# Values phase of a retention and HGRN2 step: a second plain pair, sums on DVE, tiles at multiples of 512 bytes

## The chip, the core and the metric

The kernel runs on one core of a Trainium2 chip. The core has a matrix engine (TensorE, PE in the profile), a vector engine (VectorE, DVE), a scalar engine (ScalarE, ACT), GpSimd (POOL) and an engine that here issues DMAs (SyncE, SP). Each takes its instructions strictly in the order in which they stand; they wait for each other by semaphores. The metric is the device time of one execution in microseconds, the median over runs.

## The reference

One decoder layer over a prompt of 2,048 tokens and a batch of 8 new tokens, width 1,024, in float32. The input is RMS-normalised and multiplied by `w_in` (1,024 x 4,096), whose columns are eight groups of 512: for retention q, k, v and gate, for HGRN2 q, forget gate, value and gate. Each branch has four heads of 128.

```python
h = rmsnorm(x, norm_g)
p = (h @ w_in).astype(jnp.float32)
rq, rk, rv, rg, hq, hf, hi, hgate = jnp.split(p, 8, axis=-1)
...
o_ret, s_ret_new = chunked_decay_recurrence(rq, rk, rv, log_gamma, s_ret)
o_hg, s_hg_new = chunked_decay_recurrence(hq_act, kin, hi, logf, s_hg)
...
y = x + concatenate([norm(o_ret) * silu(rg), norm(o_hg) * silu(hgate)]) @ w_out
```

Retention has rotary positions and a fixed decay per head; HGRN2 has a forget gate per token and channel. Outputs are the normalised y for prompt and new tokens and the new states.

## The kernel before

**Numbers in two parts.** Every operand of the large products is split into a rounded high part (a copy on ACT into `float32r`) and a low part (a subtraction on DVE): `hi_lo` (lines 100 to 102, and `split`). `three` (line 287) then does three matmuls, high by high, high by low, low by high, into one PSUM accumulation.

**The values phase** (lines 164 to 491, up to about 212 us) computes the two value groups, `rv` and `hi`, for all tokens and writes them to DRAM. Tokens are taken in eight pairs of 128-token chunks, in the order `V_ORDER = [4, 5, 6, 7, 2, 3, 0, 1]`. The product of a pair is a 2 x 2 block product: two token chunks, two halves of the inner dimension, two groups of columns. The first pair is done plainly, eight block products (96 matmuls of 512 columns, loop at lines 437 to 455), while the weights arrive. The other seven are done by a Strassen-Winograd scheme with seven block products (84 matmuls, `v_pair`, `PRODUCTS`), for which sums of weight blocks (T1 to T4, made once by `wv_comb` from raw tiles `wvr`, four adds per k on POOL, each then split) and sums of token blocks (S1 to S4, `tok_ops`, four adds per pair on POOL, split by `s_split`) are needed. The decode tokens' values are 32 more matmuls (`decode_values`).

**Normalisation.** `stats(i)` loads two rows of 128 x 1,024 of the prompt one after the other into the single buffer `xn`, squares and sums them on ACT, and POOL makes the inverse root (`rsqrt_mean`). A plain pair needs it only at the eviction, as a scale per row. A Strassen pair needs it along the columns: `spread(i)` builds two diagonal matrices `dg` on DVE, PE multiplies them by ones (line 236), ACT copies the result to SBUF, and `tok_ops` multiplies the transposed tokens by it.

**Buffers.** Raw loads (`rawp`, six buffers of 4 KB per partition) are shared by weights, tokens and S sums; pools are laid out in SBUF in the order in which they are opened. In the built program `xh0` begins at byte 11,168 of a partition, `xl0` at 27,808, the weight buffers `wh` at 77,728 and the first T tile at 128,320: 416, 160, 416 and 320 past a multiple of 512. A row of an x tile is 520 numbers, 2,080 bytes. The output product's `wo` tiles take the places of the x tiles, with rows of 4,096 bytes; its other operand stands in the weight buffers.

**After the values phase** come sixteen units, one per half of the tokens, branch and head: projections (line 530) with the recurrence of the unit before woven in by `merge` (line 970). `merge` takes a list of steps with weights and places each at its share of the unit's projection work; what counts is the order that comes out of it. Nothing reorders PE's instructions; on the other engines a scheduler sets the order at build time. For an HGRN head (`hgrn_rec`) the steps are `scores0`, `scores(1)`, `scores(3)`, `scores3`, then transposes of k (`k0`, `k1`, line 635), state updates (`u0`, `u1`), outputs and output transposes. Between the scores a chain runs: ACT copies k and q (`keep`, lines 764 and 765), POOL multiplies k (line 754) and DVE multiplies q (line 757) by decays, in place; `scores3` (matmuls at lines 829 and 834) reads both, and `k0` reads k after POOL's last multiplication. At the end stands the output product (line 1107), with the decode work among it (lines 911 and 953).

Of the kernel before, what the change touches and what calls it, by code (L numbers as in the profile page):

```python
# [41 lines left out]
def step_kernel(ctx, tc, a, out):  # L42
# [27 lines left out]
    pool.memset(mhalf, -0.5)  # L70

# [21 lines left out]
    rst = const.tile([P, T - 512], F32, name="rst")  # L93
    dq, dk, df, dg_ = (const.tile([P, 8, NB], F32, name=f"d{n}") for n in "qkfg")
# [74 lines left out]
    side = [xp.tile([P, KT, 512 + NB], F32R, tag=f"x{t}1", name=f"wv_{t}") for t in "hl"]  # L169
# [33 lines left out]
    def stats(i):  # L203
        p = V_ORDER[i]
        ms = sm.tile([P, 2], F32, tag="ms", name=f"ms{p}")
        for j in range(2):
            c = 2 * p + j
            if i == 1:
                r = wp.tile([P, D], F32, tag="w" + "hl"[j], name=f"xn{c}")
            else:  # L210
                r = vq.tile([P, D], F32, tag="xn", name=f"xn{c}")
            sp.dma_start(r, a["x_prompt"][0, c * P : (c + 1) * P, :])
            act.activation(r, r, AF.Square, accum_out=ms[:, j : j + 1])
        rsqrt_mean(rs_all[:, 2 * p : 2 * p + 2], ms, D, EPS)

    def stats0():
        p = V_ORDER[0]
        ms = sm.tile([P, 4], F32, tag="ms4", name="ms0", bufs=1)
        for n, tag in enumerate(("s1", "u2", "u3", "vo")):
            c, h = 2 * p + n % 2, n // 2  # L220
            r = vq.tile([P, GW], F32, tag=tag, name=f"xn0{n}", bufs=2 if tag == "vo" else 1)
            sp.dma_start(r, a["x_prompt"][0, c * P : (c + 1) * P, h * GW : (h + 1) * GW])
            act.activation(r, r, AF.Square, accum_out=ms[:, n : n + 1])
        pool.tensor_tensor(ms[:, 0:2], ms[:, 0:2], ms[:, 2:4], op=ALU.add)
        rsqrt_mean(rs_all[:, 2 * p : 2 * p + 2], ms[:, 0:2], D, EPS)

    spread_to = {}

    def spread(i):
        p = V_ORDER[i]  # L230
        pt = ps_tr.tile([P, 2, P], F32, tag="tr", name=f"prs{p}")
        for j in range(2):
            c = 2 * p + j
            dg = vq.tile([P, P], F32, tag="dg", name=f"dg{c}", bufs=2)
            dve.tensor_scalar(dg, ident, rs_all[:, c : c + 1], None, op0=ALU.mult)
            pe.matmul(pt[:, j], ones, dg, start=True, stop=True)
        if p >= 2:
            dst = rst[:, (p - 2) * 256 : (p - 1) * 256]
        else:
            dst = vq.tile([P, 256], F32, tag="rb", name=f"rb{p}", bufs=2)  # L240
# [5 lines left out]
    def tok_ops(i):  # L246
        r0, r1 = xr[i]
        rb = spread_to[i]
        for j, r in enumerate((r0, r1)):
# [5 lines left out]
            hi_lo(xh0[:, 4 * j : 4 * j + 4, slot(i)], xl0[:, 4 * j : 4 * j + 4, slot(i)], r)  # L255
# [3 lines left out]
        pool.tensor_tensor(s1, a21, a22, op=ALU.add)  # L259
        pool.tensor_tensor(s2, s1, a11, op=ALU.subtract)  # L260
        pool.tensor_tensor(s3, a11, a21, op=ALU.subtract)
        pool.tensor_tensor(s4, a12, s2, op=ALU.subtract)
# [71 lines left out]
    def tok_load0(k0, tag):  # L334
        r = vq.tile([P, GW], F32, tag=tag, name=f"x0r{k0}", bufs=2 if tag == "vo" else 1)
        x0r[k0] = r.rearrange("p (k t) -> p k t", k=2)
        sp.dma_start(x0r[k0], a["x_t"][V_ORDER[0], :, k0 : k0 + 2])

    def x_split0(k):
        h, l = xh0[:, k, :256], xl0[:, k, :256]  # L340
        r = x0r[k - k % 2][:, k % 2]
# [7 lines left out]
    def wv_load(k, cuts=1):  # L349
        wr[k] = rawp.tile([P, 2, GW], F32, tag="raw", name=f"wvr{k}")  # L350
# [86 lines left out]
    for kk in range(4):  # L437
# [5 lines left out]
        if kk == 3:  # L443
            spread(1)
# [774 lines left out]
```

## Time and profile before

| | us |
|---|---|
| three runs | 1144.94, 1144.24, 1141.24 (median 1144.24) |
| profiled execution, whole | 1144.43 |
| its span, first to last instruction | 1142.6 |
| PE busy | 1095.2 (96%) |
| DVE, ACT, POOL busy | 665.9, 377.5, 270.7 |
| granted TensorE clock, mean | 0.989 |

Times in the views are microseconds from the span's start. A row of the waits names the waiting engine, tile and line, then whom it waited for, the total, how often, and the longest. Matmuls are pipelined: one of 512 columns is shown as about 394 ns long, but the next starts some 230 ns later, so the pace is read from groups (time of a group over its count).

### The profile page before, as it was taken

To read this page: it belongs to the slowest core of one execution; us is meant where nothing else is said; L and a number is where in the kernel's file an instruction comes from. 1 tells how busy PE (TensorE), PEld (TensorE's weight loads), DVE (VectorE), ACT (ScalarE), POOL (GpSimd) and SP (SyncE) were. 2 spreads that over 40 slices of the span, in tenths; PEclk is the share of its full clock that TensorE was granted. 3 is DMA by queue.
4 is the path that set the end of the run, shared out by engine and by line. 5 is a ranking of instruction groups with operands and counts; after the bars stand their busy time and mean duration, and the time that the engine had idled before them with its cause. 6 is when DMAs were issued, how large, how long until landed. Compare 5 with 4: busy or idle time off the path is not lost.

```text
span 1142.6 us, 21543 instructions
## 1 busy us (share of the span) xinstructions
PE 1095.2 (96%) x9062; PEld 922.9 (81%) x9062; DVE 665.9 (58%) x1048; ACT 377.5 (33%) x777; POOL 270.7 (24%) x268
## 2 busy tenths in 40 slices
PE   5889899999999999999999999999999999999997
PEld 3568688898998998998988888788788878878785
DVE  7856667566447447455757644644545685566343
ACT  6553323223323233322533322332322442233311
POOL 5733342013014005103302302401410420010011
PEclk9889899999999999999999999999999999999999
DMA  6355425821220221221443122122022275777431
GB/s 247 112 181 187 138 74 156 270 84 38 74 75 21 75 65 49 74 56 40 136 142 94 40 77 75 36 69 82 26 77 58 76 199 173 214 241 234 153 126 61
DMA packets 96305, 125.77 MB, mean 110 GB/s; under 512 B 4968, under 2 KB 69736, under 8 KB 96208
## 3 DMA queue, kind: packets, MB, share of 16 engines
q1 hardware_dynamic: 96064, 124.13, 34.7%
q8 instruction: 71, 1.16, 0.4%
q10 hardware_dynamic: 144, 0.26, 0.1%
q14 instruction: 26, 0.21, 0.1%
HBM read 93.11 MB, written 31.26 MB: 109 GB/s over the span
## 4 chain that ended last, share of the span: by engine, by line
PE 63%; issue 11%; POOL 11%; DVE 7%; ACT 4%; DMA 3%; SPq 0%; POOLq 0%; DVEq 0%; ACTq 0%
PE py L1107 15%; PE pjg L530 10%; PE pjfh L530 8%; PE pv L289 8%; PE pjqh L530 8%; POOL kh L754 5%; POOL qr L585 2%; DMA xn<-in_x_prompt 2%; PE pjqr L530 2%; ACT kepth L764 2%; POOL kr L585 1%; PE pur L642 1%; PE por L657 1%; PE par L699 1%; PE por L659 1%
## 5 line engine op out<-in xcount | busy, mean ns | idle before, releaser
L530 PE MATMUL pjg<-xh,w_h 128*128 128x512 f32 (+2 forms) x320 | 116.9, 365 | 0.0
L530 PE MATMUL pjg<-xh,w_l 128*128 128x512 f32 (+2 forms) x320 | 111.9, 350 | 0.0
L530 PE MATMUL pjg<-xl,w_h 128*128 128x512 f32 (+2 forms) x320 | 111.6, 349 | 0.0
L1107 PE MATMUL py<-woh,oc_h 128*128 128x512 f32 x256 | 100.8, 394 | 0.0
L1107 PE MATMUL py<-woh,oc_l 128*128 128x512 f32 x256 | 99.8, 390 | 0.0
L1107 PE MATMUL py<-wol,oc_h 128*128 128x512 f32 x256 | 99.6, 389 | 0.0
L101 ACT ACTIVATE w_h<-wr 128x1024 fp32r<-128x1024 f32 x48 | 50.8, 1058 | 100.6 <-PE pjg L530 48.8
L757 DVE TENSOR_TENSOR qth<-qth,fph 128x512 f32<-128x512 f32 x48 | 50.7, 1057 | 44.9 <-ACT kepth L765 43.2
L102 DVE TENSOR_TENSOR w_l<-wr,w_h 128x1024 fp32r<-128x1024 f32 x48 | 62.8, 1309 | 22.2 <-ACT w_h L101 22.0
L764 ACT ACTIVATE kepth<-kh 128x1024 f32<-128x1024 f32 x24 | 25.5, 1061 | 127.4 <-POOL kh L754 127.4
L530 PEld LDWEIGHTS pjg<-xh,w_l 128*128 128x128 f32 x320 | 60.1, 188 | 8.6
L530 PEld LDWEIGHTS pjg<-xl,w_h 128*128 128x128 f32 x320 | 60.4, 189 | 6.7
L530 PEld LDWEIGHTS pjg<-xh,w_h 128*128 128x128 f32 x320 | 60.3, 188 | 6.5
L754 POOL TENSOR_TENSOR kh<-kh,fph 128x512 f32<-128x512 f32 x48 | 56.8, 1184 | 32.1 <-ACT kepth L764 28.1
L97 POOL TENSOR_SCALAR orsr<-omsr,pk 128x4 f32<-128x4 f32 x16 | 4.3, 269 | 250.9 <-ACT jkr L663 250.9
L530 PE MATMUL pjfh<-xh,w_h 128*128 128x512 f32 (+2 forms) x160 | 58.9, 368 | 0.0
L530 PE MATMUL pjkr<-xh,w_h 128*128 128x512 f32 (+2 forms) x160 | 58.4, 365 | 0.0
L530 PE MATMUL pjqr<-xh,w_h 128*128 128x512 f32 (+2 forms) x160 | 58.4, 365 | 0.0
L530 PE MATMUL pjqh<-xh,w_h 128*128 128x512 f32 (+2 forms) x160 | 57.8, 361 | 0.0
L1107 PEld LDWEIGHTS py<-woh,oc_h 128*128 128x128 f32 x256 | 48.1, 188 | 10.4
L1107 PEld LDWEIGHTS py<-woh,oc_l 128*128 128x128 f32 x256 | 48.0, 188 | 10.2
L530 PE MATMUL pjqr<-xh,w_l 128*128 128x512 f32 (+2 forms) x160 | 56.1, 351 | 0.0
(485 smaller groups left out, 2851.4 us busy)
## 6 DMA issues: line engine op xcount, KB each, us to landing
wr<-in_w_in SPq DMA_DIRECT2D x48, 512.0 KB, 4.4
v_dram<-vo SPq DMA_DIRECT2D x32, 256.0 KB, 3.1
v<-v_dram SPq DMA_DIRECT2D x16, 512.0 KB, 4.8
or<-o_dram SPq DMA_DIRECT2D x16, 512.0 KB, 5.2
xrc<-in_x_prompt SPq DMA_DIRECT2D x16, 512.0 KB, 3.8
out_y_prompt<-yc SPq DMA_DIRECT2D x15, 512.0 KB, 2.6
xn<-in_x_prompt SPq DMA_DIRECT2D x14, 512.0 KB, 4.1
xr<-in_x_t SPq DMA_DIRECT2D x14, 512.0 KB, 4.3
```

The source lines that it names most:

```text
L101: act.activation(h, src, AF.Copy)
L102: dve.tensor_tensor(l, src, h.bitcast(F32), op=ALU.subtract)
L289: pe.matmul(ps, xx, ww, start=(first and n == 0), stop=(last and n == 2))
L530: pe.matmul(ps, ww[:, kk], x[:, k, b0 : b0 + n], start=(k == 0 and i == 0), stop=(k == KT - 1 and i == 2),)
L585: pool.tensor_tensor(dst[:, tt], t1[:, :n], t2[:, :n], op=ALU.add)
L642: pe.matmul(pu[:, j], ksb[g][:, j], vcol(4 * g + j), start=True, stop=True)
L657: pe.matmul(po[:, j], A[:, c], vcol(c), start=True, stop=src is None)
L659: pe.matmul(po[:, j], qcol(c), src, start=False, stop=True)
L754: pool.tensor_tensor(kv[:, :, 0, :], kv[:, :, 0, :], two[:, :, 1:2].to_broadcast([P, nb, b]), op=ALU.mult)
L757: dve.tensor_tensor(qv[:, :, 1, :], qv[:, :, 1, :], two[:, :, 0:1].to_broadcast([P, nb, b]), op=ALU.mult)
L764: act.activation(ss[:, 512:], k[:, :HALF], AF.Copy)
L1107: pe.matmul(ps, o[:, kk], w[:, k % 4, i * 512 : (i + 1) * 512], start=(k == 0 and n == 0), stop=(k == KT - 1 and n == 2),)
```

## The change

The diff touches the values phase, the layout of tiles, and one table of weights:

- The pair after the first is plain as well (192 plain matmuls, then six Strassen pairs of 84). Its tokens come in small tiles (`tok_load0(1, k)`), and each of its four outputs is accumulated over all k in turn, with the decode values between.
- All eight raw weight tiles have a buffer of their own (two of them in the pool of the split weights). The sums of weights are no longer between the loops of the first pair; `wv_comb` comes after it, and its adds, like those of `tok_ops`, are on DVE instead of POOL. One `stats` serves the first pair like the others.
- `spread` is cut in two: `spread_dg` (diagonals on DVE) a step earlier, `spread` (matmul and copy) where it was. For the last pairs and the decode it stands in other places.
- For Strassen pairs below the sixth only the first 128 columns of the first half of x are split, since the rest is not read there.
- The pool `sm` is opened earlier, a tile `fill` of 56 numbers is added, x tiles have rows of 512 numbers (block 1: 528). In the built program `xh0` is then at byte 12,800, `xl0` at 29,184, `wh` at 79,360 and the first T tile at 128,512, all multiples of 512; rows of x are 2,048 bytes, in block 1 2,112.
- Fourteen matmuls of `ones` by `ones` into a scratch bank stand first on PE.
- The weights of the steps of an HGRN head: scores 2.4 to 2.3 each, `k0` 1.0 to 1.9, `o0`, `o1` and `t1` 0.8 to 0.7, `t0` 1.0 to 1.2. In the built program `scores3` comes 1.4 us of projection matmuls earlier in all eight heads; `k0` stands behind 18 matmuls of 512 columns (or as many columns of smaller ones) after it, where it stood behind 18 of 256 and 264 or 12 of 512.

DVE at the start of the program, from its first x split on (`x0r` raw tokens, `wvr` raw weights, `wv` the tiles B11 and B21). Before:

```order
L343 SCALAR_TENSOR_TENSOR xl_124<-x0r_142,g_in,xh_123 128x256 x2
L102 TENSOR_TENSOR wv_l<-wvr_144,wv_h 128x512
L102 TENSOR_TENSOR B12l_139<-wvr_144,B12h_137 128x512
L343 SCALAR_TENSOR_TENSOR xl_124<-x0r_147,g_in,xh_123 128x256 x2
L102 TENSOR_TENSOR wv_l<-wvr_149,wv_h 128x512
L102 TENSOR_TENSOR B22l<-wvr_149,B22h 128x512
L102 TENSOR_TENSOR T1l<-wvr_144,T1h 128x512
L102 TENSOR_TENSOR T3l<-wvr_144,T3h 128x512
L102 TENSOR_TENSOR wv_l<-wvr_164,wv_h 128x512
L102 TENSOR_TENSOR B12l_139<-wvr_164,B12h_137 128x512
L102 TENSOR_TENSOR T2l<-wvr_149,T2h 128x512
L102 TENSOR_TENSOR wv_l<-wvr_166,wv_h 128x512
```

The change, at the same place:

```order
L345 SCALAR_TENSOR_TENSOR xl_140<-x0r_159,g_in,xh_139 128x256 x2
L107 TENSOR_TENSOR wv_l<-wvr_161,wv_h 128x512
L368 TENSOR_TENSOR wvr_161<-wvr_161 128x512
L107 TENSOR_TENSOR B12l_155<-wvr_161,B12h_153 128x512
L345 SCALAR_TENSOR_TENSOR xl_140<-x0r_164,g_in,xh_139 128x256 x2
L107 TENSOR_TENSOR wv_l<-wvr_166,wv_h 128x512
L369 TENSOR_TENSOR wvr_161<-wvr_166,wvr_161 128x512
L107 TENSOR_TENSOR B22l<-wvr_166,B22h 128x512
L107 TENSOR_TENSOR T1l<-wvr_161,T1h 128x512
L370 TENSOR_TENSOR wvr_166<-wvr_166,wvr_161 128x512
L107 TENSOR_TENSOR wv_l<-wvr_181,wv_h 128x512
L107 TENSOR_TENSOR B12l_155<-wvr_181,B12h_153 128x512
```

DVE now makes the sums itself between its splits (lines 368 to 370). Up to the last operand of the first pair it has the four adds and splits of the first k and one add of the second; the other sums stand behind.

SP's queue where the statistics of the third pair are loaded (`xn` prompt rows, `xns` decode rows, `xr` raw tokens, `vo` and `vd` values on their way out). Before:

```order
L212 DMA xn_436<-in_x_prompt 128x1024
L198 DMA xr_510<-in_x_t 128x1024
L198 DMA xr_511<-in_x_t 128x1024
L198 DMA xr_529<-in_x_t 128x1024
L212 DMA xn_439<-in_x_prompt 128x1024
L283 DMA v_dram_91<-vo_444 128x512
L283 DMA v_dram_92<-vo_447 128x512
```

The change:

```order
L215 DMA xn_255<-in_x_prompt 128x1024
L284 DMA v_dram_92<-vo_390 128x512
L284 DMA v_dram_91<-vo_393 128x512
L380 DMA xns<-in_x_sample 8x1024
L284 DMA v_dram_92<-vo_396 128x512
L284 DMA v_dram_92<-vo_489 128x512
L215 DMA xn_428<-in_x_prompt 128x1024
L284 DMA v_dram_92<-vo_517 128x512
L215 DMA xn_431<-in_x_prompt 128x1024
```

The rows of the third pair (428 and 431) now stand behind those of the second (252 and 255), the decode rows and five outputs; all of them go through the one buffer `xn`.

The core of the diff:

```diff
     const = ctx.enter_context(tc.tile_pool(name="const", bufs=1))
+    sm = ctx.enter_context(tc.tile_pool(name="sm", bufs=2))
...
-    sm = ctx.enter_context(tc.tile_pool(name="sm", bufs=2))
...
+    wu = ps_tr.tile([P, P], F32, tag="tr", name="wu")
+    for n in range(14):
+        pe.matmul(wu, ones, ones, start=True, stop=True)
...
+    const.tile([P, 56], F32, name="fill")
...
     def x_alloc(blk):
+        n = 528 if blk == 1 else 512
         x_cur[blk] = tuple(
-            xp.tile([P, KT, 512 + NB], F32R, tag=f"x{t}{blk % 2}", name=f"x{t}{blk}") for t in "hl"
+            xp.tile([P, KT, n], F32R, tag=f"x{t}{blk % 2}", name=f"x{t}{blk}") for t in "hl"
         )
...
-            hi_lo(xh0[:, 4 * j : 4 * j + 4, slot(i)], xl0[:, 4 * j : 4 * j + 4, slot(i)], r)
+            n = P if i < 6 and j == 0 else 2 * P
+            at = slice((i % 2) * 256, (i % 2) * 256 + n)
+            kk = slice(4 * j, 4 * j + 4)
+            hi_lo(xh0[:, kk, at], xl0[:, kk, at], r[:, :, :n])
...
-        pool.tensor_tensor(s1, a21, a22, op=ALU.add)
...
+        dve.tensor_tensor(s1, a21, a22, op=ALU.add)
...
     def wv_load(k, cuts=1):
-        wr[k] = rawp.tile([P, 2, GW], F32, tag="raw", name=f"wvr{k}")
+        pl, tag = {3: (wp, "wh"), 7: (wp, "wl")}.get(k, (rawp, "raw"))
+        wr[k] = pl.tile([P, 2, GW], F32, tag=tag, name=f"wvr{k}")
...
-        pool.tensor_tensor(r0[:, 0], r0[:, 1], r0[:, 0], op=ALU.subtract)
...
+        dve.tensor_tensor(r0[:, 0], r0[:, 1], r0[:, 0], op=ALU.subtract)
...
+    for k in (0, 4, 2, 6):
+        tok_load0(1, k)
     sp.dma_start(pk, a["pack"])
+    stats(1)
+    decode_inputs()
+    for k in range(KT):
+        x_split0(1, k)
     pv0 = {(c, ty): bank([P, GW], f"pv0{c}{ty}") for c in range(2) for ty in range(2)}
     for kk in range(4):
...
-        wv_comb(kk)
...
+    wv_comb(0)
+    wv_comb(1)
+    tok_load(2)
+    stats(2)
+    wv_comb(2)
+    wv_comb(3)
+    spread_dg(2)
+    for ty in (1, 0):
+        for c in range(2):
+            ps = bank([P, GW], f"pv1{c}{ty}")
+            for k in range(KT):
+                plain_k(1, ps, c, ty, k, k == 0, k == KT - 1)
+            plain_out(1, c, ty, ps)
+            if (c, ty) == (0, 0):
+                spread(2)
+                tok_ops(2)
+                s_split(2, 0)
+                stats(3)
+        decode_values(ty)
...
-    for i in range(1, N_V):
+    for i in range(2, N_V):
...
-        steps = [(0.3, scores0), (2.4, lambda: scores(1)), (2.4, lambda: scores(3)), (2.4, scores3)]
-        steps += [(1.0, t["k0"]), (0.9, t["u0"]), (0.2, t["k1"]), (0.9, t["u1"]), (0.8, t["o0"]),
-                  (0.8, t["o1"]), (1.0, t["t0"]), (0.8, t["t1"]), (0, last)]
+        steps = [(0.3, scores0), (2.3, lambda: scores(1)), (2.3, lambda: scores(3)), (2.3, scores3)]
+        steps += [(1.9, t["k0"]), (0.9, t["u0"]), (0.2, t["k1"]), (0.9, t["u1"]), (0.7, t["o0"]),
+                  (0.7, t["o1"]), (1.2, t["t0"]), (0.7, t["t1"]), (0, last)]
```

More of the change, by code (lines that the diff above doesn't have):

```diff
@@ L168, in step_kernel @@
     xh0, xl0 = x_cur[0]
-    side = [xp.tile([P, KT, 512 + NB], F32R, tag=f"x{t}1", name=f"wv_{t}") for t in "hl"]
+    side = [xp.tile([P, KT, 528], F32R, tag=f"x{t}1", name=f"wv_{t}") for t in "hl"]
     Bop = {}
@@ L214, in stats, with spread_dg @@
         rsqrt_mean(rs_all[:, 2 * p : 2 * p + 2], ms, D, EPS)
[L216 to L225, printed above, removed]
-    spread_to = {}
+    spread_to = {}
+    dgs = {}
+    def spread_dg(i):
+        dgs[i] = []
+        for c in (2 * V_ORDER[i], 2 * V_ORDER[i] + 1):
+            dg = vq.tile([P, P], F32, tag="dg", name=f"dg{c}", bufs=2)
+            dve.tensor_scalar(dg, ident, rs_all[:, c : c + 1], None, op0=ALU.mult)
+            dgs[i].append(dg)
     def spread(i):
@@ L231, in spread @@
         pt = ps_tr.tile([P, 2, P], F32, tag="tr", name=f"prs{p}")
[L232 to L235, printed above, removed]
+        for j, dg in enumerate(dgs[i]):
             pe.matmul(pt[:, j], ones, dg, start=True, stop=True)
```

127 lines of the change are left out of this document (58 added, 69 removed).

## The prediction

> **What bounds the kernel now.** I read the page's engine totals first (PE 1095.2 of 1142.6 us), then the busy time by stretch, cut where PE's groups begin or break off:
>
> ```profile
> 6.50:44.60 38.10, 29.74 (x101) 22.02 (x102) 37.75 (x43) 24.05 (x49) 25.66 (x18) 0.91 0.56 200
> 44.60:66.10 21.50, 14.79 (x57) 9.02 (x54) 11.89 (x18) 11.21 (x21) 12.38 (x13) 0.90 0.54 170
> 66.10:89.00 22.90, 22.84 (x88) 18.52 (x89) 14.79 (x25) 9.52 (x14) 7.90 (x6) 0.87 0.54 176
> 121.00:130.00 9.00, 3.66 (x11) 2.91 (x10) 7.02 (x8) 5.37 (x7) 6.98 (x4) 0.63 0.39 135
> 130.00:211.70 81.70, 81.70 (x357) 65.86 (x356) 57.32 (x88) 24.71 (x31) 20.17 (x14) 1.00 0.41 133
> 211.70:936.00 724.30, 711.00 (x7391) 617.97 (x7390) 410.50 (x718) 230.33 (x537) 167.16 (x156) 1.00 0.25 77
> ```
>
> Columns: stretch, its length, busy us (instructions) of PE, PE's weight loads, DVE, ACT, POOL, then granted clock, DMA share, GB/s. From 130 us on PE is full. Ahead of that it is idle for 8.4, 6.7 and 5.3 us in three stretches, the granted clock falls below 1 beside each, and in the first DVE is busy 37.75 of 38.10 us. So the values phase is bound by what feeds PE, and the rest by PE. Who is waited for:
>
> ```profile
> PE pv L289 <- ACT wv_h L101: 10.3, 3, 6.6
> PE prs L236 <- DVE dg L235: 8.4, 2, 5.3
> PE pkh L635 <- POOL kh L754: 5.5, 6, 1.3
> PE pv L289 <- DVE wv_l L102: 4.6, 4, 1.6
> PE pv L289 <- ACT vo L463: 3.7, 1, 3.7
> ```
>
> Lines 289 and 236 are the first phase (27.0 us of waits, 6.6 of them for the first operand); 635 are the transposes of the HGRN heads. The pace of an undisturbed PE comes from the chain of waits (start, us, group):
>
> ```profile
> 177.65 0.45 PE prs L236 x4
> 178.09 33.63 PE pv L289 x144
> 211.73 5.59 PE pjfh L530 x24
> 989.10 17.71 PE py L1107 x78
> 1115.85 7.40 PE pyd L953 x32
> ```
>
> A 512-column matmul takes 33.63/144 = 233.5 ns in the values phase, 5.59/24 = 232.9 in the projections, 227.1 in the output product, 231.3 in the decode product with the same moving tiles as the output product.
>
> **1. PE's work in the values phase.** Before: 96 (plain pair) + 7 x 84 + 32 (decode) = 716 matmuls, 167.2 us at 233.5 ns. After: 2 x 96 + 6 x 84 + 32 = 728, 170.0 us: the second plain pair costs 2.8 us. Eight spreads of 0.45 us and the small decode one add 3.8. The phase ran from 6.6 to 211.7 us, so 205.1 - 167.2 - 3.8 = 34.1 us are waits and half clock. That is all the first part can win.
>
> **2. The feed of the first pair.**
>
> ```profile
> 11.22 0.68 DVE L102 TENSOR_TENSOR B22l<-wvr,B22h 128x512 fp32r<-128x512 f32 x1
> 11.82 0.68 DVE L102 TENSOR_TENSOR T1l<-wvr,T1h 128x512 fp32r<-128x512 f32 x1
> 12.04 1.60 POOL L367 TENSOR_TENSOR wvr<-wvr,wvr 128x512 f32<-128x512 f32 x1 [1.63 <-DVE B22l L102]
> 12.42 1.77 DVE L102 TENSOR_TENSOR T3l<-wvr,T3h 128x512 fp32r<-128x512 f32 x1
> 5.62 0.88 DVE L343 SCALAR_TENSOR_TENSOR xl<-x0r,g_in,xh 128x256 fp32r<-128x256 f32 x2 [4.75 <-ACT xh L342]
> 8.93 0.61 ACT L101 ACTIVATE B22h<-wvr 128x512 fp32r<-128x512 f32 x1
> 5.00:10.00 5.00, 3.44 (x7) 2.44 (x8) 4.03 (x6) 4.35 (x9) 2.60 (x2) 1.00 1.02 390
> ```
>
> With POOL quiet, DVE starts one 512-column subtraction every 0.60 us (11.22 to 11.82); the one that runs beside POOL's add takes 1.77. The change takes POOL's adds away, so DVE's adds are priced at 0.60 (bounds 0.60 and 1.60, POOL's own). In the new order DVE has, up to the last operand of pair 0, sixteen weight splits, four splits of sums and five adds (25 x 0.60) and four pairs of x splits (0.88): 18.5 us from 5.6, so 24.1. ACT is not later: twenty copies of at most 0.61, eight x rows of half the width and one square of 1.16 (its row is below). Weights no longer queue behind raw buffers: eight tiles, 5.8 MB with the x rows and one statistics load ahead of the last, at 390 GB/s are in by about 18 us. PE needs 96 x 0.2335 = 22.4 us; it is now PE that ends last.
>
> **3. The dummies and the start.**
>
> ```profile
> 8.30 0.63 PE L289 MATMUL pv<-wv_h,xh 128*128 128x512 f32 x1
> 8.73 0.63 PE L289 MATMUL pv<-wv_l,xh 128*128 128x512 f32 x1
> 66.16 1.19 PE prs L236 x4
> ```
>
> The first matmuls come 0.43 us apart, half speed, until about 10.7 us. Fourteen dummies of two passes take between 28 x 0.11 = 3.1 us (the 0.45 us for four above) and 28 x 0.26 = 7.2 (four in 1.19 at the low clock) from about 1.1 us on: PE is free between 4.2 and 8.3, first operand at 6.6. I take 7.2 at full clock. Pair 0 then ends at 7.2 + 22.4 = 29.6; it ended at 44.6.
>
> **4. The second pair and the wait that replaces the others.** Pair 1 needs no row statistics, only eight x splits that stand behind the 24.1 on DVE, done by 29. Its 96 and the decode's 32 run from 29.6. After 48 + 16 + 24 of them, at 29.6 + 88 x 0.2335 = 50.1, PE comes to the spread of pair 2, and that needs pair 2's statistics. These come one by one through the single buffer `xn`:
>
> ```profile
> 105.98 4.89 DMA xn<-in_x_prompt
> 110.95 1.16 ACT xn L213 x2
> 112.13 4.05 DMA xn<-in_x_prompt
> 116.26 1.15 ACT xn L213 x2
> ```
>
> One load and square: 4.05 to 4.89 + 1.16, about 5.4 us. The first square stands on ACT behind the copy for T4, which waits for DVE's fifth add at about 17.3 by the prices above: it ends at 19.1; five more loads and the small `xns` between (about 4) give 19.1 + 27 + 4 = 50.1, POOL and DVE 1.4: 51.5. ACT's queue adds up to 1 (squares wait behind evictions). So PE waits 1.5 to 2.5 us, and a wait over 3 us has cost half clock behind it (the 5.3 us one, clock 0.63). I take 3.0, bounds 0 and 10 (if each load takes 5.5 and each square finds ACT taken). Behind the diagonal on DVE stand pair 2's scaling and sums; by these prices they end at about 66, and PE wants them only at 68.8, after decode and two products. From there on the chain is ahead of PE. DVE's work in a pair is then eight scalings (3.5), four sums (2.4, new here), low parts of 4,096 columns (4.8), seven evictions (4.2) and two diagonals: 15.5 of the 20 us that PE takes.
>
> Phase end: 7.2 + 170.0 + 3.8 + 3.0 = 184.0 against 211.7: **-27.7** (bounds -33 and -19).
>
> **5. Rows and tiles at multiples of 512 bytes.** Output product: moving and stationary rows lie at 416 or 160 past a multiple of 512, equal modulo 256, and 227.1 ns. Decode product: same moving tiles, stationary rows of 160 bytes, so all remainders: 231.3. Values: T tiles at 320 against stationary at 416: 233.5. Projections: moving rows step 2,080 bytes, every remainder: 232.9. After the change nearly all are at 0, as equal as the output product's. Bounds: nothing, and the whole way to 227.1. I take the latter, the row it resembles most. Which matmuls:
>
> ```profile
> L530 PE MATMUL pjg<-xh,w_h 128*128 128x512 f32 x192 | 79.6, 415 | 0.0
> L530 PE MATMUL pjqh<-xl,w_h 128*128 128x512 f32 x96 | 37.8, 393 | 0.0
> ```
>
> Three operand pairs of the gate (x192) and of four other projections (x96): 1,728, x 5.8 ns = 10.0 us. The 256- and 264-column ones read block 1, whose rows become 2,112 bytes: nothing. Values phase: 728 x 6.4 = 4.7. Where the HGRN chain sets the pace (point 6) some 1.2 come back as waits: **-13.5**.
>
> [...]
>
> **6. The later transposes.** One head of the second half, in time order:
>
> ```profile
> 635.02 1.06 POOL L754 TENSOR_TENSOR kh<-kh,fph 128x512 f32<-128x512 f32 x1 [1.17 <-ACT kepth L764]
> 635.52 0.70 PE L829 MATMUL plh<-kepth 128*32 128x32 f32 x32
> 635.50 1.14 DVE L757 TENSOR_TENSOR qth<-qth,fph 128x512 f32<-128x512 f32 x1 [2.04 <-ACT kepth L765]
> 636.78 1.12 PE L834 MATMUL plh<-qth,kh 128*64 128x64 f32 x16 [0.56 <-DVE qth L757]
> 640.47 1.04 POOL L754 TENSOR_TENSOR kh<-kh,fph 128x512 f32<-128x512 f32 x1
> 641.57 0.66 PE L635 MATMUL pkh<-ident,kh 128*128 128x128 f32 x4 [0.68 <-POOL kh L754]
> ```
>
> The chain runs through ACT, DVE and POOL; PE waits for it at 834 and at 635. The new weights do two things in all eight heads: the last scores (829, 834) come 1.4 us of projections (six matmuls of 512) earlier, and the transposes stand 4.2 us of projections behind them instead of 2.1 to 2.8. In the heads that wait like this one (three) scores wait 1.4 longer and the 1 us at the transposes goes: +0.4 each. In heads one to three the transposes also move back 0.7 and their waits of up to 1.3 go for 1.3 at the scores: -0.1 each. Heads four and eight do not wait at the transposes now:
>
> ```profile
> 544.62 1.12 PE L834 MATMUL plh<-qth,kh 128*64 128x64 f32 x16 [0.52 <-DVE qth L757]
> 547.90 0.60 PE L635 MATMUL pkh<-ident,kh 128*128 128x128 f32 x4
> ```
>
> they only gain the wait: +1.4 and +1.1. Together **+3.4** (bounds: -5.5, all waits of 635 gone and none new; +11.2, 1.4 new in all eight).
>
> **Sum.** 1142.6 - 27.7 - 13.5 + 3.4 = 1104.8 us of span. The profiled execution took 1144.43, 1.8 outside the span, and the median of the runs is 1144.24, 0.2 less; so 1.6 goes on top: **1106.4 us**, say 1106.
>
> **Rivals.** (a) The remainders don't matter: 1142.6 - 27.7 + 3.4 + 1.6 = 1120. For it: 227.1 might belong to the output stage for another reason. Against: the decode product in that same stage. [...] (b) The statistics chain or DVE is later than worked: 10 us instead of 3 at the spread of pair 2, and a second such wait of 5 with half clock at pair 3: 1106 + 12 = 1118, or 1132 with (a) too. For it: the two waits for `dg` now, 8.4 us. Against: those came with POOL's adds ahead of the scaling on every pair. (c) Equal remainders collide: if moving row and weight load come from the same bank on every matmul, each 512-column one gets dearer, the output product's 768 too: 1,728 + 728 + 768 and 1,152 half ones, 3,800 in all. The other terms win 24.3 us, so from 6.4 ns each the gain is gone and from 7.3 it is a loss past 0.3%; at 10 ns the time is 1144.2 - 24.3 + 38 = 1158. For it: pace that depends on rows at all. Against: the output product has equal remainders and is the fastest. (d) 227.1 is itself held up by the 32 bytes that its rows lie off a multiple of 64, and all go below it: at 220 ns another 3,200 x 7 = 22 us, 1084.
>
> **Chances.** Forecast 0.53 (own range 1099 to 1113), (a) 0.25, (b) 0.12, (c) 0.05, (d) 0.05. Range 1096 to 1123: the forecast's own, (a) with 3 us of spread and half of (b). A measurement of this kernel tells 0.3% (3.4 us) from no change; only (c) reaches that side: faster 0.94, same 0.03, slower 0.03.
>
> **What would show it.** First projection (`pjfh`) at about 179 us with the fast pace, 184 without; pair 0's last matmul near 29 us, no PE wait over 1 us ahead of the spread of pair 2, and one of 1 to 4 there. Twenty-four `pjfh` in 5.45 us. No PE wait for POOL's `kh` at the transposes, and a larger one for `qth` and `kept` at the scores, about 16 us in sum. It would be wrong if DVE's adds ran over 0.7 us, if the projections stayed at 232 ns, or if PE waited for a `dg` in more than one pair.

## The result, and the profile after

The change took the median from 1143.59 us (four runs, 1141.24 to 1144.94) to **1112.70 us** (four runs, 1110.74 to 1114.57): a ratio of 0.973, 95% interval 0.970 to 0.976. The profiled execution is the shortest of the four, 1110.74 us with a span of 1108.9.

The kernel after, busy time by stretch, cut where PE's groups begin or break off (columns as in the prediction):

```profile
0.00:6.43 6.43, 5.05 (x28) 4.86 (x28) 0.98 (x4) 3.21 (x7) 0.89 (x8) 1.00 0.56 173
6.43:28.96 22.53, 22.30 (x96) 17.87 (x97) 22.50 (x43) 19.75 (x41) 1.44 (x2) 1.00 0.86 320
28.96:49.34 20.38, 20.38 (x90) 15.29 (x88) 14.11 (x27) 13.80 (x27) 3.35 (x5) 1.00 0.59 196
49.34:55.80 6.46, 3.36 (x11) 2.90 (x11) 2.19 (x7) 2.22 (x5) 0.90 (x2) 0.74 0.38 125
55.80:182.22 126.42, 126.42 (x570) 103.43 (x570) 100.48 (x166) 48.81 (x68) 4.96 (x10) 1.00 0.53 174
182.22:902.55 720.33, 704.83 (x7393) 620.45 (x7393) 402.73 (x717) 232.64 (x539) 176.86 (x156) 1.00 0.25 77
902.55:1108.90 206.35, 199.26 (x920) 160.34 (x919) 105.76 (x118) 56.67 (x97) 18.09 (x40) 1.00 0.54 171
```

PE's three stretches of waiting in the values phase have become one, from 49.34 to 55.80, where the granted clock is 0.74. In pair 0 (second row) DVE is busy 22.50 of 22.53 us, so it is still full, but PE is now full too and no longer waits for it. The stage ends are 182.2 and 902.6 us. Before, they were 211.7 and 936.4 (the first `py` group of before starts at 936.38). So the values phase gave 29.5 us, the projections with the recurrences took 720.3 instead of 724.6 us (4.3), and the output stage 206.4 instead of 206.2.

PE's waits after:

```profile
PE plh L851 <- ACT kepth L787: 9.7, 5, 2.4
PE prs L234 <- DVE dg L227: 3.1, 1, 3.1
PE plh L856 <- DVE qth L779: 2.4, 7, 0.6
PE poth L694 <- DVE oth L696: 2.1, 2, 1.7
```

Lines after are those of before plus 22 (851 and 856 are the last scores, 829 and 834 before). The waits for weights (0.5 us in sum are left) and for POOL's `kh` at the transposes are gone; one wait for a diagonal `dg` stays. At the last scores PE waits 9.7 us for `kept`, where it waited 1.3.

Pace, from the chain of waits (start, us, group):

```profile
182.22 5.44 PE pjfh L552 x24
881.63 1.39 PE pjqr L552 x6
906.17 2.76 PE py L1129 x12
913.03 4.12 PE py L1129 x18
926.26 5.45 PE py L1129 x24
955.26 17.73 PE py L1129 x78
```

The undisturbed projections run at 5.44/24 = 226.7 ns (232.9 before). A group of six behind other work takes 231.7 ns each; groups of 12, 18, 24 and 78 of the output product take 230.0, 228.9, 227.1 and 227.3.

### The profile page after: what moved, and what is told of

It is laid out like the page before. It is cut to its first block, busy times and chain, and to the rows that moved or that the text cites. A ratio compares the mean times of both kernels' runs of the same rounds, so it can differ in the third digit from the quotient of the medians.

```text
span 1108.9 us, 21594 instructions
## 1 busy us (share of the span) xinstructions
PE 1081.6 (98%) x9102; PEld 925.1 (83%) x9102; DVE 648.8 (59%) x1077; ACT 377.1 (34%) x780; POOL 206.5 (19%) x223
## 4 chain that ended last, share of the span: by engine, by line
PE 72%; issue 11%; POOL 8%; ACT 4%; DMA 2%; DVE 2%; POOLq 0%; DVEq 0%; ACTq 0%; SPq 0%
PE py L1129 16%; PE pv L290 11%; PE pjg L552 9%; PE pjfh L552 8%; PE pjqh L552 8%; PE pjkr L552 4%; POOL kh L776 4%; PE pjqr L552 2%; POOL qr L607 2%; ACT kepth L786 2%; DMA xn<-in_x_prompt 1%; PE pur L664 1%; PE puh L664 1%; PE par L721 1%; PE por L679 1%
## 5 line engine op out<-in xcount | busy, mean ns | idle before, releaser
L107 DVE TENSOR_TENSOR w_l<-wr,w_h 128x1024 fp32r<-128x1024 f32 x48 | 59.7, 1244 | 23.8 <-ACT w_h L106 23.3
L1129 PEld LDWEIGHTS py<-woh,oc_h 128*128 128x128 f32 x256 | 48.1, 188 | 10.4
L1129 PEld LDWEIGHTS py<-woh,oc_l 128*128 128x128 f32 x256 | 48.0, 188 | 10.2
L1129 PEld LDWEIGHTS py<-wol,oc_h 128*128 128x128 f32 x256 | 48.1, 188 | 9.7
L552 PE MATMUL pjfh<-xh,w_l 128*128 128x512 f32 (+2 forms) x160 | 55.7, 348 | 0.0
```

The costliest lines, as they stand in the source:

```text
L107: dve.tensor_tensor(l, src, h.bitcast(F32), op=ALU.subtract)
L552: pe.matmul(ps, ww[:, kk], x[:, k, b0 : b0 + n], start=(k == 0 and i == 0), stop=(k == KT - 1 and i == 2),)
L1129: pe.matmul(ps, o[:, kk], w[:, k % 4, i * 512 : (i + 1) * 512], start=(k == 0 and n == 0), stop=(k == KT - 1 and n == 2),)
```

## The experiments

Times are medians beside runs of the kernel before on the same chip, 1144.04 to 1144.92 us. "Middle" is the stretch from the first `pjfh` to the first `py`, 720.3 us in the changed kernel and 724.6 before; "values" the stretch from the first real matmul to the first `pjfh`, 175.6 and 205.0. Both are worked out from the starts of matmuls in the traces. The four runs of the changed kernel spread over 3.8 us, so a difference of some 3 us from its median is no more than that spread, and for such differences the traces decide.

### What the tile layout is worth

**The layout taken back** in the changed kernel:

```diff
-        n = 528 if blk == 1 else 512
+        n = 520
...
-    const.tile([P, 56], F32, name="fill")
...
-    sm = ctx.enter_context(tc.tile_pool(name="sm", bufs=2))   # ahead of xp
+    sm = ctx.enter_context(tc.tile_pool(name="sm", bufs=2))   # behind rawp
```

> The changed kernel with the tile layout of before (x rows of 520 numbers, the small pool behind the raw buffers, no fill); everything else of the change stays. By the forecast's point 5 the layout is worth 13.5 us, so 1126 us and 512-column matmuls of the projections at 232 to 233 ns everywhere. By the trace of the changed kernel it is less: the projections there run at 231 ns for the first six to ten 512-column matmuls after other work on PE and at 227 only behind them, 228.2 in the mean, so 2,456 matmuls x 4.4 ns = 10.8, less what comes back as waits at the scores (1 to 2): 1121 to 1123. By rival (a), where the rows don't matter and the pace changed for another reason: 1113.

Measured 1115.89 us (1114.23 to 1119.27, five runs): only 3.2 more than with the layout. The projections are back at the old pace everywhere (232.5 to 232.7 ns). So the rows do matter to the pace (rival (a) falls), but much of what they gain at the matmuls does not reach the end: the projection matmuls take 6.3 us more than with the layout, the middle only 3.1 (723.3). PE's waits in this run:

```profile
PE plh L850 <- ACT kepth L786: 8.9, 5, 2.2
PE prs L233 <- DVE dg L226: 1.3, 1, 1.3
```

The values phase takes 175.5 us, as long as with the layout. A slower PE comes later to the diagonal, waits 1.3 us instead of 3.1, and has no half clock behind it.

**The layout alone**, put into the kernel before (same edit the other way round).

> The kernel before with the new tile layout alone (all operand tiles at multiples of 512 bytes, x rows of 2,048). Forecast's point 5: 1143.6 - 13.5 = 1130. With the first matmuls after other work still at 231 ns: 1143.6 - 10.8 + 1 to 2 = 1134 to 1135. Rows don't matter: 1144. If the layout only pays together with the new values phase, the projections stay at 232 to 233 ns here.

Measured 1138.00 us, ratio 0.9947 (0.9934 to 0.9961): 6.0 us, less than half of the forecast. Middle 721.5 instead of 724.6, values 203.4 instead of 205.0.

**Where the 5.8 ns went.** The table has the mean start-to-start time of 512-column matmuls in the projections, by how many of them PE has done since other work (recurrence, transposes), in ns:

| | 1st to 3rd | 4th to 10th | later |
|---|---|---|---|
| before | 232.0 | 232.6 | 232.5 |
| layout taken back | 232.5 | 232.7 | 232.7 |
| after | 231.7 | 228.7 | 226.7 |

With the layout the pace only comes in after a few matmuls, and the recurrence's steps break the projections into pieces: about six in ten stand at one of the first ten places. Over 1,607 projection matmuls followed by another one the sum falls from 384.7 to 378.1 us: 4.1 ns each, not 5.8.

### What in the layout counts

The base of these three is the fastest kernel below (`half_steps`), whose PE hardly waits. The edit is one more tile behind the x tiles, or a larger fill:

```diff
     side = [xp.tile([P, KT, 528], F32R, tag=f"x{t}1", name=f"wv_{t}") for t in "hl"]
+    xp.tile([P, 24], F32, tag="pad", name="pad")     # 96 bytes; 16 numbers for 64 bytes
...
-    const.tile([P, 56], F32, name="fill")
+    const.tile([P, 64], F32, name="fill")            # the third: all tiles 32 bytes on
```

> half_steps with 96 bytes between the x tiles and all that lies behind them: weights, S and T operands stand at 96 past a multiple of 512, x and the wo tiles at 0. If equal remainders are what counts, products of two shifted operands (S2 x T2, S3 x T3, S1 x T1, S4 x B22) keep 227 ns, while A22 x T4, the projections and the output product, which pair a shifted operand with an unshifted one, go to 231 to 234 ns in the middle of long runs: 1,607 x 4 + 808 x 5 + some 150 x 5 ns = 11 us more, 1112. If each operand must lie on a multiple of 64 for itself, the shifted pairs slow down too: 1114. If only rows that step off 512 bytes (2,080 before) cost, nothing changes: 1101.

Measured 1112.68 us against 1101.02 without the shift. Within the last pair, stretches from the first matmul of a product to the first of the next: S3 x T3, S1 x T1 and S4 x B22 (both operands shifted), then A22 x T4 (x not shifted). The counts are twelve and the end of the one before:

```profile
167.82:170.54 2.72, 2.72 (x13) 1.00 0.86 300
170.54:173.26 2.72, 2.72 (x13) 1.00 0.86 291
173.26:175.99 2.73, 2.73 (x13) 1.00 0.87 257
175.99:178.79 2.80, 2.80 (x13) 1.00 0.84 244
```

Equal remainders keep 226.7 ns, also at 96 past a multiple of 512; the unequal product takes 233 ns with nothing else changed around it. The projections and the output product, which now pair shifted with unshifted tiles, from the chain of the same run:

```profile
178.96 5.63 PE pjfh L556 x24
953.06 18.28 PE py L1133 x78
```

234.6 and 234.4 ns: the output product, untouched by the change so far, loses its 227.

> As the run with 96 bytes, with 64: the shifted tiles then stand on multiples of 64, not of 128. If a grain of 64 bytes counts, 1101 and 227 ns everywhere; if the remainder modulo 128 or more, as with 96 bytes: 1110 to 1112.

Measured 1110.64 us. Chain:

```profile
178.48 5.60 PE pjfh L556 x24
951.34 18.21 PE py L1133 x78
```

233.3 and 233.5 ns. So a remainder that differs by 64 costs nearly as much as one by 96: the grain is larger than 64 bytes. It is at most 256, since the output product of before ran at 227.1 with rows at 416 and 160 past a multiple of 512.

> half_steps with every tile 32 bytes further (fill of 64 numbers): remainders equal to each other but 32 past a multiple of 64. Forecast's rival (d) and the reading by absolute place say that this alone changes the pace (the output product of before lay so and took 227.1): equal remainders: 1101 and 227 ns; absolute multiples of 64 needed: 231 to 234 ns and 1110.

Measured 1102.33 us (1101.10 to 1102.77) against 1101.02 (1100.28 to 1102.20), with spans of 1099.0 and 1098.9; the first 24 projections:

```profile
177.42 5.44 PE pjfh L555 x24
```

So it is the remainder of one operand against the other that counts, not where each lies. That leaves nothing of rival (d): 227 is not held up by the 32 bytes.

### The statistics of pair 2

The chain that ends at the wait, in the changed kernel:

```profile
32.80 5.47 DMA v_dram<-vo
39.91 0.68 ACT vo L424
40.59 1.03 ACT xns L382 x2
41.63 3.34 DMA xn<-in_x_prompt
46.23 3.45 DMA xn<-in_x_prompt
51.27 0.72 POOL rs_all L103
52.01 0.30 DVE dg L227
52.45 1.19 PE prs L234 x4
```

Pieces in between, `issue` among them, are left out. The earlier loads and squares of the chain went through the same buffer from 19.2 us on; between them and these rows the chain passes once through ACT's queue, which was held by the store of an evicted value (first row).

**Loads in halves through two buffers:**

```diff
-        for j in range(2):
-            r = vq.tile([P, D], F32, tag="xn", name=f"xn{c}")
-            sp.dma_start(r, a["x_prompt"][0, c * P : (c + 1) * P, :])
-            act.activation(r, r, AF.Square, accum_out=ms[:, j : j + 1])
+        for n in range(4):
+            c, h = 2 * p + n % 2, n // 2
+            r = vq.tile([P, GW], F32, tag="xn", name=f"xn{c}{h}", bufs=2)
+            sp.dma_start(r, a["x_prompt"][0, c * P : (c + 1) * P, h * GW : (h + 1) * GW])
+            act.activation(r, r, AF.Square, accum_out=ms[:, n : n + 1])
+        pool.tensor_tensor(ms[:, 0:2], ms[:, 0:2], ms[:, 2:4], op=ALU.add)
```

> The changed kernel with the rows for the statistics loaded in halves of 512 columns through two buffers of 2 KB instead of whole through one of 4 KB (decode rows too), so that a load runs beside the square of the one before. Forecast's point 4: PE waits at the spread of pair 2 for a chain of six loads and squares through one buffer, 5.4 us each. Then here that wait (3.1 us, and 1.2 of half clock behind it) is gone, the values phase ends 3 to 4.5 us earlier, at 177.5 to 179, and the time is 1108 to 1109.5. Rival: what is late is DVE (sums and scaling of pair 2) and not the loads; then PE waits as long at the spread or at the product with S2, and the time stays at 1112 to 1113. Third: SP's queue, where the halves stand ahead of evicted values, holds the evictions and PE waits at the banks.

Measured 1110.07 us (1106.17 to 1111.38). In the values phase the forecast's reading holds:

```profile
PE prs L235 <- DVE dg L228: 0.2, 1, 0.2
```

The phase ends at 178.1 us, and takes 171.1 instead of 175.6 us: in the profiled execution the wait and its half clock cost 4.5. The size differs from execution to execution. In the profiles of the two runs below that change only the step weights, PE waits 3.3 us there with 6.8 us of half clock behind it (the phase takes 176.4) and 1.9 us with none (172.8). In the profile with halved loads 2.3 of it are lost again in the middle (722.5 us), whose instructions are the same. Where, the stretch shows (same columns as above):

```profile
687.18:694.01 6.83, 6.36 (x42) 5.27 (x35) 3.32 (x5) 2.38 (x6) 2.54 (x3) 0.50 0.01 4
```

Half clock, behind the last scores of the sixth head. The changed kernel has it at the same heads, sixth and seventh:

```profile
682.00:690.70 8.70, 6.70 (x151) 5.09 (x149) 6.57 (x8) 2.52 (x4) 4.89 (x4) 1.00 0.20 62
690.70:694.12 3.42, 2.87 (x48) 2.72 (x48) 3.05 (x4) 2.60 (x7) 0.93 (x1) 0.50 0.02 7
782.86:786.27 3.41, 2.86 (x48) 2.72 (x48) 3.04 (x4) 2.60 (x7) 0.92 (x1) 0.50 0.00 0
```

There PE waits 2.4 us for `kept`, with small matmuls around the wait: 32 of 32 columns and 16 of 64 behind it. In the run with the layout taken back the longest of these waits is 2.2, and no half clock is granted in its middle. In the kernel before, waits of 3.7, 3.1 and 5.3 us end at 58.5, 66.2 and 126.5 us, and half clock is granted from 58.46 to 61.87, from 65.28 to 72.11 and from 123.31 to 130.14; the waits that were enough here are shorter.

The length of a wait does not decide alone. At the fifth head of the changed kernel a wait of 2.38 us has no half clock behind it, and in the run without the dummies (next) one of 1.40 at the fourth head, with smaller ones around it, has. The traces show what goes with all of them. In each trace, the half-clock stretches begin whole multiples of 3.413 us apart (52.41, 690.70 and 782.86 us in the changed kernel: 187 and 27 of them; 27.74, 37.98, 58.46, 65.28 and 123.31 us in the one before: 3, 6, 2 and 17). PE had been idle for 56% or more of the 3.413 us just before each (at these places 59 to 90% in the changed kernel, 62 to 100% in the one before). At full clock and behind the first 10 us, stretches of that grid with up to 52% idle, and two of 56% near the program's end, have no half clock behind them. The wait at the fifth head falls half into one such stretch and half into the next, those at the sixth and seventh lie in one for 2.0 us. So whether a wait costs half clock goes with how it lies on this grid, which stands at another place in every trace. This is read from the fourteen traces afterwards; no run was made to test it.

### The dummies

**Left out** (the fourteen matmuls of `ones`).

> The changed kernel without the fourteen dummy matmuls. The first real matmuls then run at half clock until about 3.4 us after the start of PE's work: pair 0 ends 1.7 us later, at about 31. What happens behind it tells the two readings apart: if the statistics chain sets the time of the spread of pair 2 (forecast's point 4), PE only waits 1.5 us less there and the time is 1112 to 1113; if PE sets it, the whole delay stays: 1114 to 1115.

Measured 1111.94 us (1111.52 to 1112.97, four runs), against 1112.70 with them. Chain:

```profile
6.40 35.47 PE pv L286 x144
51.04 0.67 PE prs L230 x4
```

The first eleven matmuls start about 0.43 us apart, half pace, and the last of pair 0 starts at 30.6 instead of 28.9 us. The 3.4 us of the expectation are 3.5 in the trace of the changed kernel, where the dummies' matmuls start 0.21 us apart up to 4.6 us (PE's first at 1.1) and 0.11 from then on; here eleven times 0.43 make some 4.7. But at the spread of pair 2 PE finds its diagonal ready: no wait, no half clock, and the values phase ends at 179.1, 3 us earlier than with the dummies. The diagonal is also there earlier, at 50.9 us instead of 52.3: the load issued at 30.8 and its square took 5.3 us in this profile, 7.1 (from 30.6) in the one with the dummies. Why stays open. The dummies buy 1.7 us that the wait for the statistics chain takes back. The middle is 3.9 us longer in this profile (724.1 us), with a third half-clock stretch, at the fourth head.

### Sums on POOL again

```diff
-        dve.tensor_tensor(r0[:, 0], r0[:, 1], r0[:, 0], op=ALU.subtract)
+        pool.tensor_tensor(r0[:, 0], r0[:, 1], r0[:, 0], op=ALU.subtract)
...
-        dve.tensor_tensor(s4, a12, s2, op=ALU.subtract)
+        pool.tensor_tensor(s4, a12, s2, op=ALU.subtract)
```

(all eight adds of `wv_comb` and `tok_ops`)

> The changed kernel with the sums of weights and of tokens on POOL again. Forecast's point 2: POOL's adds take 1.60 us and DVE's subtraction beside one 1.77 instead of 0.60 to 0.68. Five adds before the end of pair 0 would cost DVE about 5 x 1.1 us, with pair 0 ending 3 to 6 us later; the fifth add also gates the square of pair 0's rows and with it the statistics of pair 2: PE waits 6 to 10 us instead of 3.1 at its spread and the values phase ends 4 to 9 us later: 1117 to 1122. If POOL costs DVE nothing here since DVE has room: 1112 to 1114.

Measured 1130.98 us (1129.51 to 1135.26), 18.3 more and outside what was expected. Waits, then groups on DVE and POOL from 6.4 to 29 us (busy, mean ns of one):

```profile
PE prs L234 <- DVE dg L227: 9.3, 3, 5.8
PE pv L290 <- DVE wv_l L107: 6.0, 4, 2.4
```

```profile
L107 DVE TENSOR_TENSOR T3l<-wvr,T3h 128x512 fp32r<-128x512 f32 x2 | 3.6, 1778 | 0.0
L345 DVE SCALAR_TENSOR_TENSOR xl<-x0r,g_in,xh 128x256 fp32r<-128x256 f32 x7 | 7.2, 1067 | 0.0
L368 POOL TENSOR_TENSOR wvr<-wvr 128x512 f32<-128x512 f32 x3 | 5.0, 1675 | 8.4 <-DVE wv_l L107 8.4
```

In the changed kernel, same stretch:

```profile
L345 DVE SCALAR_TENSOR_TENSOR xl<-x0r,g_in,xh 128x256 fp32r<-128x256 f32 x14 | 6.0, 481 | 0.0
L368 DVE TENSOR_TENSOR wvr<-wvr 128x512 f32<-128x512 f32 x2 | 1.4, 688 | 0.0
```

Beside POOL's adds the x splits slow down too, from 481 to 1067 ns, not the subtractions alone on which the expectation rested; the subtractions that no add overlaps stay at 680 ns (eight of them up to 40 us). The last matmul of pair 0 starts at 40.3 us instead of 28.9, and the phase has two stretches of half clock of 6.8 us each. So 18.3 of the 31 us that the change gains hang on the place of the adds. The values phase takes 194.3 us here, 205.0 in the kernel before: the other 10.7 come from the rest of the change there (the second plain pair, the weights' own buffers, the earlier diagonals and others) and were not taken apart.

### The later transposes

**The old step weights back** in the changed kernel, then a middle way (scores where they stood before, transposes later, taken from the output steps):

```diff
-scores 2.3 each, k0 1.9, u0 0.9, k1 0.2, u1 0.9, o0 0.7, o1 0.7, t0 1.2, t1 0.7
+scores 2.4 each, k0 1.0, u0 0.9, k1 0.2, u1 0.9, o0 0.8, o1 0.8, t0 1.0, t1 0.8
...
+scores 2.4 each, k0 1.9, u0 0.9, k1 0.2, u1 0.9, o0 0.5, o1 0.5, t0 1.0, t1 0.5
```

> The changed kernel with the HGRN step weights of before (scores 2.4 of 13.9, first transposes right behind them). Forecast's point 6: the later transposes cost 3.4 us, so 1109.3 here, PE's waits for POOL's kh come back at the transposes (5 to 7 us) and the wait for kept at the last scores falls from 9.7 to about 2. By the pitch of PE in the two traces (excess at scores and transposes 12.4 us before, 14.7 after) it costs 2.3: 1110.4. If the waits only move and their sum is the same: 1112.7.

> The changed kernel with scores at their places of before and the first transposes 18 matmuls behind the last scores (scores 2.4 of 13.9, k0 1.9, taken from the output steps). If the forecast's reading of the chain holds, both waits are small: no wait for kh at the transposes and 2 to 4 us in sum for kept and qth at the scores, so 14.7 - 6 = 8 to 9 us less than now: 1104 to 1106. If waits go to the output steps that stand closer together (oth, A copies), 2 to 4 come back: 1107 to 1110. If the chain through ACT, DVE and POOL sets the pace of the unit whatever the places, 1112.

The old weights: 1112.45 us (1109.41 to 1113.00). The waits move, as told (`kh` back, `kept` down), and the sum is the same:

```profile
PE pkh L657 <- POOL kh L776: 5.7, 6, 1.3
PE plh L851 <- ACT kepth L787: 3.1, 3, 1.0
```

The middle way: 1107.43 us (1105.76 to 1107.88). Of the 3.0 us between the two profiled executions (spans 1105.9 and 1108.9) 2.8 lie in the values phase, which the step weights do not touch (1.9 us of wait and no half clock), and 0.6 in the middle (719.6). So this run does not show that the middle way as such gains 5 us. No wait for `kh`, but at the output transposes, which stand closer behind the outputs:

```profile
PE poth L694 <- DVE oth L696: 4.0, 4, 2.6
```

**Both** the halved statistics and a third set of weights (scores 2.4, k0 1.4, u0 0.8, u1 0.8, o0 and o1 0.6, t0 1.2, t1 0.8):

> Statistics in halves as in the run beside this one, and in the HGRN heads the scores at their places of before with the first transposes 15 matmuls behind them (k0 1.4, taken from u and o steps; the steps from the second transposes on stand as in the changed kernel). If the waits of the changed kernel at the last scores (kept 9.7, qth 2.4) come from the scores' earlier place alone, they fall to 3 to 5 in sum and no wait comes at the transposes: another 6 to 7 us, 1102 to 1104. If the 15 matmuls are too few, waits for kh come back: 1105 to 1107. If waits are handed on to the outputs: 1107 to 1109.

Measured **1101.02 us** (1100.28 to 1102.20, five runs), ratio to before 0.9624 (0.9610 to 0.9638): it beats both kernels. In the traces 4.6 us of the gain over the changed kernel are in the values phase and 6.2 in the middle (714.1). Its waits in the middle, all sums above 0.6 us:

```profile
PE plh L854 <- ACT kepth L790: 3.0, 3, 1.0
PE plh L859 <- DVE qth L782: 2.4, 5, 0.6
PE poth L697 <- DVE oth L699: 2.3, 2, 1.8
PE poth L697 <- DVE dq L892: 0.9, 1, 0.9
```

Fifteen to eighteen matmuls between the last scores and the first transpose are enough, and no half clock is left before the end. Time from the first matmul of an HGRN head's recurrence to the first of the next retention head's, in us (the last one spans part of the output stage):

| head | 1 | 2 | 3 | 4 | 5 | 6 | 7 | 8 |
|---|---|---|---|---|---|---|---|---|
| before | 49.7 | 50.3 | 50.2 | 51.9 | 49.8 | 50.4 | 50.4 | 50.9 |
| old weights | 49.6 | 50.1 | 50.1 | 51.2 | 50.3 | 50.5 | 50.4 | 51.1 |
| after | 48.2 | 48.3 | 48.3 | 52.4 | 50.7 | 51.6 | 51.6 | 51.6 |
| both | 48.1 | 48.4 | 48.4 | 51.9 | 49.3 | 49.4 | 49.4 | 51.5 |

Against the old weights, those of the change gain 1.4 to 1.9 us in each of the first three heads and lose 0.3 to 1.2 in each of the others. With the scores back at their places and the transposes still later (last row), the first three keep their gain and heads five to seven are 1 us better than with the old weights: in these heads it is the earlier scores that lose, with the half clock behind them at heads six and seven.

**The layout taken back where nothing waits**, in the fastest kernel:

> The kernel with halved statistics and scores in their old places (half_steps, 1101.0), with the tile layout of before. There PE hardly waits, so what the layout gives can't come back as waits. By the traces so far (projections 1,607 matmuls x 4.0 ns, values phase some 700 x 4.6, output product unchanged): 6.4 + 3.3 = 9.7, so 1110 to 1111. By the forecast's price (5.8 and 6.4 ns for 1,728 and 728): 14.7, so 1115 to 1116. If also here only the 3.2 us are lost that rows_back lost against the changed kernel (1112.7 to 1115.9), the time is 1104, and the gain of the layout goes somewhere that no wait shows.

Measured 1107.65 us (1107.30 to 1108.45): 6.6 more than 1101.02, not the 9.7 worked out. Chain:

```profile
180.91 5.58 PE pjfh L554 x24
952.05 17.73 PE py L1131 x78
```

The pace is that of before, 232.5 ns, and the output product keeps its 227.3. Values are 2.9 us longer and the middle 4.1, where its projection matmuls alone take 6.4 more. Of the other 2.3, 1.5 come back as shorter waits of PE (8.7 us in sum instead of 10.2): the chain of the recurrence through ACT, DVE and POOL does not run faster with PE. Where the rest went, no wait shows.

## Why the prediction was right, and where not

The forecast was 1106 us, range 1096 to 1123; the measured 1112.7 lies 6.7 above it, inside the range. The span of the profiled run is 1108.9 against 1104.8: 2.9 of the 4.1 in the values phase, 1.0 in the middle, the rest in the output stage and rounding. The median stands another 2.0 above the profiled execution: two of the four runs took 1110.8, two 1114.5. Why is open; half-clock stretches, which differ from profile to profile, are a candidate. The mean granted clocks, in order of time, are 0.995, 0.992, 0.991 and 0.991.

**Point 1, PE's work.** Held: 728 matmuls, and the 34 us of waits and half clock were what the first part could win. 4.5 of them are left in the profiled execution, by the run with halved loads.

**Point 2, the feed of pair 0.** Held. The last matmul of pair 0 starts at 28.9 us ("near 29"), PE waits at most 0.3 us ahead of the spread, and DVE's adds take 688 ns each in a row of instructions that starts every 0.6. With the adds on POOL again pair 0 ends 11.4 us later and the kernel takes 18.3 us more, so they were the larger part of the cause. The part of the weights' own buffers and of the second plain pair was not tested.

**Point 3, the dummies.** The size was on the safe side: in this profile they end at 6.2 and the first real matmul starts at 6.4, not 7.2; in the other profiles with dummies it starts at 6.7 to 7.1. What the sum did not hold: the 1.7 us that they bring at pair 0 are not on the path that sets the end, since point 4's chain does not start earlier for them. The time is the same without them (1111.94).

**Point 4, the statistics of pair 2.** The mechanism was right: with the halved loads the wait is gone. PE arrived at 49.3 (50.1 forecast), the diagonal came at 52.3 (51.5). The cost was 4.5 us, not 3.0: 3.1 of wait and 1.4 of half clock behind it, for which the term had left half a microsecond. That the two add up to 4.5 is this execution: the other profiles of the same values phase lie 1.7 and 5.3 above the one with halved loads.

**Point 5, the layout.** The term was mis-sized three ways. Per matmul it measured 4.1 ns in the projections instead of 5.8, because the pace of the output product only comes in after some ten undisturbed matmuls and most of the projections stand in shorter pieces. The row that was extrapolated, a group of 78, was the least like them. Second, the values phase was priced at the full 4.7 on top of point 4's wait; but up to the spread a chain of loads sets the time, and there a faster PE only waits longer. Third, the recurrence gave back 2 to 3 us instead of 1.2. The layout's worth in this kernel is 3.2 us, in the kernel before 6.0, in the fastest 6.6, and 13.5 was forecast. That the remainders matter is shown: 96 bytes between the operands cost 7 to 8 ns on each matmul (234.6 against 226.7, 234.4 against 227.3). What in the hardware makes the difference, no run shows.

**Point 6, the later transposes.** The term was wrong: +3.4 forecast, and the old weights run as fast (1112.45; middle 721.0 against 720.3). The step that failed is the first three heads, priced at -0.1 each: their transposes lost waits of up to 1.3 us, but the scores did not get them as new ones (at most 0.2), so that they gained 1.4 to 1.9; 0.6 to 0.7 of that in each head no wait shows. In heads six and seven the loss was larger than the 0.4 forecast (1.1 each), and there half clock stands behind the wait; in head five, with the same wait and no half clock, it was 0.3. That these errors cancelled is luck; and so is that points 5 and 6 together came out near the mark in the middle (-5.4 forecast, -4.3 measured: 3.6 from the layout, 0.7 from the weights).

**The signs named in advance.** Right: 24 `pjfh` in 5.44 us (5.45), no wait for `kh` at the transposes, one wait of 1 to 4 us at the spread. Wrong: first `pjfh` at 182.2 instead of 179, and 13.2 us of waits for `kept` and `qth` at the scores instead of 16. **Rivals.** (a) falls by the pace, though the time lies halfway to it; (c) and (d) fall by the runs with shifted tiles, and a bank in which operands collide, as (c) supposed, no run shows; of (b) the half-clock part was true, without a second wait.

## What to carry to other kernels

A gain per instruction counts only where that instruction sets the end: price it per stage, and ask of each stage which chain of loads or other engines it runs against. A price read off a long undisturbed group did not hold for short pieces (here 226.7 ns against 231.7 at the first three places); look for a row that is broken up in the same way. When a step in a woven order is moved, work out the wait at every place it leaves and every place it comes to, head by head, and read the granted clock behind each.

## What the runs showed of the hardware that was not expected

- In these runs float32r matmuls of 512 columns in undisturbed stretches run at 226.7 ns when the moving rows and the stationary rows lie at equal remainders, wherever that is (0, 32 or 96 past a multiple of 512), and at 233 to 235 ns when they differ by 64 or 96 bytes. What makes the difference stays open.
- The faster pace is not there at once: 231.7 ns for the first three matmuls behind other work, 228.7 up to the tenth, 226.7 from then on. With unequal remainders the place makes no such difference (232.0 to 232.7 in the projections).
- In each trace the half-clock stretches begin on a grid of 3.413 us, behind a stretch of that grid in which PE was idle for 56% or more. So a wait of 2.4 us among small matmuls cost half clock at two heads and not at a third, and one of 1.4 did once. A half-clock stretch inside the program lasts 3.41 us or twice that (6.83), and 512-column matmuls in it start 427 ns apart (68.0 to 71.8 us of the kernel before).
- Beside POOL's adds DVE's operations of 128 x 256 and 128 x 512 took 1067 and up to 1778 ns in the mean of a group instead of 481 and 685. The subtractions that no add overlapped stayed at 680. Why DVE is slower there, no run shows.
